# A two-layer streaming step on one core: eight state buffers, gate loads on GpSimd's queue, and two of four output shares beside the second layer's heads

## The chip, the cores and the metric

The kernel runs on one core of a Trainium2 chip. The metric is the time of one execution on the device, in microseconds; less is better. The core has TensorE (matrix products), VectorE, ScalarE and GpSimd, and queues from which transfers are issued; this kernel issues them from SyncE (SP) and from GpSimd. In the profile PE is TensorE's matmuls, PEld its weight loads, DVE is VectorE, ACT is ScalarE, POOL is GpSimd.

## The reference

Two streams of tokens go through two layers with the same weights: a prompt of 512 tokens, and 8 running sequences with 16 new tokens each, 640 tokens in all, 2048 wide, in float32. Layer 0 is stick-breaking attention with 16 heads; layer 1, where most of the change lies, is gated linear attention (GLA) with 4 heads, keys 256 wide and values 512 wide. Its core, cut:

```python
def gla_chunk(S, inp):
    q, k, v, g = inp                                   # g = log of the decay
    b = jnp.cumsum(g, axis=1)
    b_last = b[:, -1]
    q_in = q * jnp.exp(b)
    a = jnp.einsum('bchd,bshd->bhcs', q_in, k * jnp.exp(-b))
    a = jnp.where(tril, a, 0.0)
    o = jnp.einsum('bhcs,bshe->bche', a, v) + jnp.einsum('bchd,bhde->bche', q_in, S)
    S = jnp.exp(b_last)[..., None] * S + jnp.einsum('bshd,bshe->bhde', k * jnp.exp(b_last[:, None] - b), v)
    return S, o
...
    o = o * lax.rsqrt(jnp.mean(o * o, axis=-1, keepdims=True) + EPS) * g_out
    y = (o.reshape(B, T, nv) * jax.nn.silu(r)).astype(h.dtype) @ w_out
...
        x = x + gate[:, None] * y
    return rmsnorm(x, final_norm_g), ...
```

The 8 running sequences start from a given state (8 x 4 heads x 256 x 512 floats, 16.8 MB), which is read, used and written back updated. The prompt starts from zero, and its last state is an output too.

## The kernel before

**Products in three parts.** Each float32 factor is split into a high part (a cast to the matmul's reduced float32, on ScalarE) and a low part (the rest, by a subtraction on VectorE): `halves`, L134 to L136. A product is then three matmuls: high by high, high by low, low by high. A weight piece of 128 x 1024 is loaded into one of two raw buffers (`wraw`, tag `wr`) and split into one of three pairs `wh`, `wl` (`split`, L140; the third pair comes from a pool of its own at every third call, counted by `ring3["n"]`).

**Who sets the order.** TensorE's order is that of the program text. The text is made by a small planner: a main product is a generator that yields every few matmuls, and at each yield `Side.tick` (L305) lets side lanes run, which are generators too. A lane says with `step(wait, tp=...)` how many planned microseconds it wants to wait and how many PSUM banks it needs; planned time (`pe["now"]`) advances with the matmuls written. `side.after(wait, what)` puts a call, a transfer mostly, on a list of due calls, which is served from its head. The order on the other engines and on the queues is chosen by the compiler's scheduler, except in a stretch around the end of layer 0 and the start of layer 1 (L1157 to L1271), where VectorE, ScalarE and GpSimd follow the text as well. `load` and `store` (L70, L73) issue on SP's queue, `move` (L76) on GpSimd's.

**Layer 0's output product** is cut into four shares, one for each four of the 16 row blocks of the contraction (`share`, L603). A share goes through four columns of 512. In a column, tokens 0 to 2 are accumulated one after the other over both weight pieces (w0 and w1), then tokens 3 and 4 side by side. `made()` (L630) splits the next raw piece: before, the second piece of a column is split at the start of that column (L635), the first piece of the next one right after. Shares 0 to 2 add into `y_t`; share 3 (L1162) adds the residual, stores x1, and squares for the norm.

**Layer 1's projections.** `six` (L434) makes head 0's values in six token tiles; its first weight piece is loaded when it is first run (L1199), after the last token's norm. `add_up` (L408) makes the sums of activation quarters that the seven-product scheme (`by_sevens`, L456) needs; two of its four subtractions run on GpSimd.

**The heads' stage** (L1281 to L1658). The main product is first `others` (L1308), the queries and keys of heads 2 and 3: 768 matmuls of 320 columns. Beside it run four lanes. `decays` (L1390) turns the gate's projection into exponentials and scales q and k of a head. `prompt_lane` (L1444) runs 16 units, 4 heads by 4 chunks of 128 tokens: attention within the chunk (L1350), transposed keys (L1485), the incoming state S times a decay, split into S1h and S1l for both halves of the key width (L1489 to L1494), the output o (L1504 to L1507), its norm, the update of S (L1509 to L1517), and, two steps into the next unit, the turned and gated rows (`leave`, L1378: transposes at L1382, the gate's product, a move to `og_d`). `sample_lane` (L1545) does the 8 sequences for each head: 16 state tiles of 128 x 512 in four groups of four. For each group there are four products with the states (L1597), then four updates (L1603, L1605), whose left factors `kst` are brought together by moves through DRAM; each state is then moved out and the next one asked for (`leaves`, L1540: after 1.5 planned us, and 3.0 more). There are S0 = 5 state buffers and, for the prompt's gates, GP = 1. `fetches` (L1613) loads the finished rows of a head, four row blocks of 128 x 640, and splits them into `og1`.

When `others` is done, the shares of layer 1's output product run as filler between the lanes' steps: share g needs the rows of head g. Shares 0 to 2 run in the heads' stage (L1652), where the third one ends after the lanes.

**The tail** (L1661 to L1731) is share 3: 240 matmuls in groups of tokens (0, 1, 2), (3,), (4,) over all four columns, with all its weights split ahead into buffers of their own; then `add` (L1679): y added, times the layer's gate, plus x1, squared, times the final norm's weights (on GpSimd, L1688, in columns 0 to 2), and in the last column the norm of the token and its stores. `hs_gemm512` (L340) is a product over several row blocks, all five tokens accumulating at once; it stands in the file and isn't called.

Of the kernel before, what the change touches and what calls it, by code (L numbers as in the profile page):

```python
# [15 lines left out]
P = 128  # L16
# [17 lines left out]
S0 = 5  # L34
GP = 1
# [6 lines left out]
def hybrid_step_kernel(ctx: ExitStack, tc: tile.TileContext, A: dict, O: list):  # L42
# [391 lines left out]
    def six(h, w, n0, acc, until, asked):  # L434

        src = w.rearrange("(kt p) n -> p kt n", p=P)
# [5 lines left out]
        nxt = piece(0)  # L442
        for j in range(8):
# [159 lines left out]
    def share(g, og, w, leave=None, at=None, first=None):  # L603
# [29 lines left out]
        w0 = made()  # L633
        for c in range(4):
            ws = [w0, made()]  # L635
# [475 lines left out]
    with tc.tile_pool(name="o0", bufs=1, reuse_waits="tile") as po, ExitStack() as only_d:  # L1111
# [51 lines left out]
        ring3.update(pool=None, tags=("wh", "wl"))  # L1163
        side.finish()
# [27 lines left out]
        acc = [bank("mm") for _ in range(5)] + [bank("z")]  # L1192

        def until(j):
            make(j + 1)
            if j == 6:
                halves(wa[:, :, :16], wa[:, :, 16:], r)

        drive(six(h2, w_in1, 2 * NK, acc, until, lambda: None))  # L1199
# [72 lines left out]
        more.close()  # L1272
        ring3["pool"] = only_d.enter_context(tc.tile_pool(name="w2", bufs=1, reuse_waits="tile"))
# [18 lines left out]
    with tc.tile_pool(name="gl", bufs=1, reuse_waits="tile") as gl:  # L1292
# [37 lines left out]
        kst = [gl.tile([P, 4, 256], F32R, name=f"kst{n}") for n in range(2)]  # L1330
# [59 lines left out]
        def decays():  # L1390

            for h in range(GH):
# [15 lines left out]
                yield step(2.0)  # L1408
# [35 lines left out]
        def prompt_lane():  # L1444
# [16 lines left out]

            def leave_left():
# [6 lines left out]
            for u, (h, c) in enumerate(units):  # L1469
# [18 lines left out]
                if c:  # L1488
                    s1h, s1l = (gl.tile([P, 2, 512], F32R, tag=n, name=n) for n in ("S1h", "S1l"))  # L1489
                    s1 = [(s1h[:, dt, :], s1l[:, dt, :]) for dt in range(2)]  # L1490
                    for dt in range(2):
                        act(s1[dt][0], S[:, dt, :], AF.Copy, scale=e1[:, dt, c:c + 1])
                        dve.scalar_tensor_tensor(s1[dt][1], S[:, dt, :], e1[:, dt, c:c + 1],
                                                 s1[dt][0].bitcast(F32), op0=ALU.mult, op1=ALU.subtract)  # L1494
# [6 lines left out]
                yield step(6.0, tp=1)  # L1501
# [3 lines left out]
                if c:  # L1505
                    for dt in range(2):
                        mm3(o, [x[:, dt, :] for x in qc], s1[dt], False, dt == 1)  # L1507
# [13 lines left out]
                yield step(4.0)  # L1521
# [237 lines left out]
```

## Time and profile before

| | us |
|---|---|
| median of 3 runs | 2677.25 |
| the runs | 2669.66, 2677.41, 2677.25 |
| the profiled execution | 2672.06 |
| its span, first to last instruction | 2670.3 |
| PE busy, PEld busy | 2491.7, 2164.2 |
| DVE, ACT, POOL busy | 1617.4, 1018.9, 268.3 |
| heads' stage, first to last matmul | 2099 to 2583 |
| tail, to the end | 2583 to 2670 |

A row of the profile that groups instructions names the line, the engine, the operation, what is written and read, and a count; then the busy time, the mean of one, and the idle time of that engine just before them with its causes. A row of waits reads: engine, tile and line that waited, what ended the wait, the total in us, how often, the longest. A row of a timeline is the start, the length, engine, line and count, and in brackets the idle time ahead of it. PE's busy time is no measure of work by itself, since matmuls overlap.

### The profile page before, as it was taken

The page shows a single profiled execution, that of the slowest core. Times are in us where ns is not written, and L with a number is a line of the kernel's source. Part 1 is how long each engine was busy: PE and PEld are TensorE (multiplying, and loading weights), DVE is VectorE, ACT ScalarE, POOL GpSimd, SP SyncE. Part 2 cuts the span into 40 slices and gives each one's busy share as a digit, 9 for nine tenths or more (in the row PEclk, how much of TensorE's full clock was granted, in tenths as well). Part 3 has the DMA queues.
Part 4 walks back from the last instruction along what each step waited for, and adds up shares of the span by engine and source line. Part 5 has one row for each costly group of instructions (what it writes and reads, how often), then busy time and mean ns, then how long its engine had stood idle before and what let it go on. Part 6 is the DMA issues. An engine that isn't in the chain of part 4 may idle for free.

```text
span 2670.3 us, 43803 instructions
## 1 busy us (share of the span) xinstructions
PE 2491.7 (93%) x17393; PEld 2164.2 (81%) x17393; DVE 1617.4 (61%) x2426; ACT 1018.9 (38%) x1804; POOL 268.3 (10%) x516
## 2 busy tenths in 40 slices
PE   6989999999999989999999889999999998788986
PEld 4569999989999988777777667999999987566765
DVE  4555555555556646667775566666676563556557
ACT  4332222222223335665442353333333552543323
POOL 1200000000000000000000052000000233233113
PEclk8899999999999999999999889999999999899998
DMA  9966666766674366667665533334434667576444
GB/s 320 313 205 214 223 203 213 228 208 212 211 225 132 115 227 221 215 213 249 198 209 155 155 109 93 112 112 136 136 104 119 200 212 243 178 233 211 168 150 166
DMA packets 503552, 503.84 MB, mean 189 GB/s; under 512 B 25706, under 2 KB 426482, under 8 KB 503218
## 3 DMA queue, kind: packets, MB, share of 16 engines
q1 hardware_dynamic: 487986, 451.74, 53.9%
q0 software_dynamic: 15360, 49.30, 5.6%
q8 instruction: 137, 2.24, 0.4%
q14 instruction: 69, 0.57, 0.1%
HBM read 411.16 MB, written 89.78 MB: 188 GB/s over the span
## 4 chain that ended last, share of the span: by engine, by line
PE 72%; DMA 11%; DVE 7%; issue 5%; POOL 2%; ACT 2%; SPq 1%; POOLq 0%; ACTq 0%; DVEq 0%
PE ps_mm L518 40%; PE ps_mm L617 11%; PE ps_mm L452 4%; PE ps_mm L573 3%; PE ps_tp L972 2%; DMA s<-in_state_gla_dram 1%; DMA ar<-in_w_ada_dram 1%; PE ps_tp L940 1%; SPq L71 1%; PE ps_z L916 1%; PE ps_z L218 1%; DVE wl L136 1%; PE ps_z L178 1%; PE ps_tp L1017 1%; PE ps_z L985 1%
## 5 line engine op out<-in xcount | busy, mean ns | idle before, releaser
L518 PE MATMUL ps_mm<-sums,wh 128*128 128x320 f32 x2880 | 643.4, 312 | 4.3 <-ACT wh L135 4.3
L518 PEld LDWEIGHTS ps_mm<-sums,wh 128*128 128x128 f32 x2880 | 480.3, 188 | 16.3 <-issue 9.1
L518 PE MATMUL ps_mm<-h,wh 128*128 128x320 f32 x2160 | 483.2, 312 | 2.6 <-DVE u L524 2.0
L518 PE MATMUL ps_mm<-sums,wl 128*128 128x320 f32 x1440 | 446.4, 310 | 1.2 <-DVE wl L136 1.2
L136 DVE TENSOR_TENSOR wl<-wr,wh 128x1024 fp32r<-128x1024 f32 x195 | 240.8, 1236 | 234.3 <-ACT wh L135 233.6
L518 PEld LDWEIGHTS ps_mm<-h,wh 128*128 128x128 f32 x2160 | 359.1, 188 | 18.9 <-issue 11.3
L135 ACT CAST wh<-wb 128x1024 fp32r<-128x1024 f32 x180 | 188.9, 1049 | 463.7 <-PE ps_mm L518 387.3
L135 ACT CAST wh<-wr 128x1024 fp32r<-128x1024 f32 x195 | 204.3, 1049 | 374.5 <-PE ps_mm L518 199.3
L518 PE MATMUL ps_mm<-h,wl 128*128 128x320 f32 x1080 | 334.2, 309 | 0.7 <-DVE wl L136 0.7
L518 PEld LDWEIGHTS ps_mm<-sums,wl 128*128 128x128 f32 x1440 | 270.8, 188 | 1.8 <-DVE wl L136 1.8
L136 DVE TENSOR_TENSOR wl<-wb,wh 128x1024 fp32r<-128x1024 f32 x180 | 220.1, 1223 | 62.4 <-ACT wh L135 62.2
L617 PE MATMUL ps_mm<-wh,ogh 128*128 128x512 f32 x530 | 231.5, 437 | 21.7 <-ACT ogh L135 14.7
L617 PE MATMUL ps_mm<-wl,ogh 128*128 128x512 f32 x530 | 212.4, 401 | 1.3 <-DVE wl L136 1.3
L617 PE MATMUL ps_mm<-wh,ogl 128*128 128x512 f32 x530 | 211.8, 400 | 0.6 <-DVE ogl L136 0.4
L573 PE MATMUL ps_mm<-h,wh 128*128 128x320 f32 x896 | 209.7, 322 | 2.4 <-DVE out L524 2.4
L518 PEld LDWEIGHTS ps_mm<-h,wl 128*128 128x128 f32 x1080 | 202.8, 188 | 1.0 <-DVE wl L136 1.0
L573 PEld LDWEIGHTS ps_mm<-h,wh 128*128 128x128 f32 x896 | 153.7, 194 | 14.8 <-issue 10.6
L617 PEld LDWEIGHTS ps_mm<-wh,ogh 128*128 128x128 f32 x530 | 102.6, 193 | 52.8 <-ACT ogh L135 15.9
L573 PE MATMUL ps_mm<-h,wl 128*128 128x320 f32 x448 | 141.3, 315 | 3.9 <-DVE wl L136 3.9
L452 PE MATMUL ps_mm<-wh,h 128*128 128x512 f32 (+1 forms) x320 | 113.1, 424 | 13.8 <-ACT wh L135 5.9
L617 PEld LDWEIGHTS ps_mm<-wh,ogl 128*128 128x128 f32 x530 | 101.9, 192 | 25.0 <-DVE ogl L136 1.8
L617 PEld LDWEIGHTS ps_mm<-wl,ogh 128*128 128x128 f32 x530 | 102.6, 194 | 16.0 <-DVE wl L136 2.1
(296 smaller groups left out, 3811.4 us busy)
## 6 DMA issues: line engine op xcount, KB each, us to landing
ar<-in_w_ada_dram SPq DMA_DIRECT2D x160, 512.0 KB
wb<-in_sb_w_in_dram SPq DMA_DIRECT2D x84, 512.0 KB
kc<-in_cache_sb_k_dram SPq DMA_DIRECT2D x64, 512.0 KB
vc<-in_cache_sb_v_dram SPq DMA_DIRECT2D x64, 512.0 KB
wb<-in_gla_w_in_dram SPq DMA_DIRECT2D x51, 512.0 KB
wr<-in_gla_w_in_dram SPq DMA_DIRECT2D x45, 512.0 KB
wr<-in_sb_w_in_dram SPq DMA_DIRECT2D x44, 512.0 KB
ar<-in_w_ada_dram SPq DMA_DIRECT2D x64, 256.0 KB
```

The costliest lines, as they stand in the source:

```text
L71: nc.sync.dma_start(out=out, in_=in_)
L135: nc.scalar.copy(hi, x)
L136: dve.tensor_tensor(lo, x, hi.bitcast(F32), op=ALU.subtract)
L178: mm(acc[32 * q:32 * q + 32, :w], cT[:, kt + m, :], by(cT[:, kt + m, :], rs[m // each][:, m % each, q, :]), start=kt + m == 0, stop=kt + m ...
L218: mm(acc[32 * j:32 * j + 32, :256], cT[:, kt + m, :], by(cT[:, kt + m, :], r[:, 256 * j:256 * j + 256]), start=kt + m == 0, stop=kt + m == ...
L452: mm(acc[i][:n, :], l, by(l, r[:, e, :]), start=j == 0 and e == 0 and first, stop=j == 7 and e == 1 and last)
L518: mm(acc, l[:, k, :], by(l[:, k, :], r), start=start and k == 0 and first, stop=k == 7 and last, skip_group_check=True)
L573: mm(acc[nt], l[:, k, :], by(l[:, k, :], r), start=k0 == 8 and k == 0 and first, stop=k0 == 0 and k == 7 and last)
L617: mm(acc, l, by(l, r[:, e, :]), start=i == 0 and e == 0 and first, stop=i == 1 and e == 1 and last)
L916: mm(z[:, :n], q[:, hh, qs], by(q[:, hh, qs], k[:, hh, :n]), start=True, stop=True)
L940: mm(o[:, :P], l, by(l, aT[:, kb, :]), start=kb == 0, stop=kb == qb)
L972: turn_block(tp[:, P * c:P * c + P], block(kc[:, c, P * hh:P * hh + P]), ident)
```

## The change

Six edits, in the order of the file.

1. `share` (both layers): the second weight piece of the next column is split right after the first piece's products of tokens 3 and 4, not at the next column's start.
2. `six` yields once after its first piece; for layer 1 it is created and run to that point ahead of `side.finish()`, so the piece's load and split stand earlier. One of `add_up`'s two GpSimd subtractions goes to VectorE, and the count of the weight ring is set before the seven-product scheme.
3. Heads' stage, buffers and queues: S0 = 8, GP = 2; gates are loaded with `move` (GpSimd's queue) instead of `load` (SP's). S1h, S1l and kst are half as large: the second half of S1 is made after the first half's products, and kst's second half is moved in after the first two groups. States are asked for in the order in which the groups now come, 8.0 instead of 3.0 planned us after their store was due.
4. Steps of the lanes are changed: in `decays` ahead of L1417 5.0 for 2.0; in the sample lane ahead of L1573 6.0 for 3.0; in a prompt unit ahead of o 4.0 for 6.0, at its end 0.5 for 4.0, and a new 3.0 between the halves of S1.
5. Two shares instead of three in the heads' stage; `fetches` brings 14 of 16 row blocks.
6. The tail accumulates the last two heads' rows (row blocks 8 to 15) at once: columns 0 to 2 by `hs_gemm512`, the last one token by token with its weights split ahead; all of `add`'s products are on VectorE.

```diff
-S0 = 5
-GP = 1
+S0 = 8
+GP = 2
...
         nxt = piece(0)
+        yield
         for j in range(8):
...
-        w0 = made()
+        w0, w1 = made(), made()
         for c in range(4):
-            ws = [w0, made()]
+            ws = [w0, w1]
             if c < 3:
                 raws += [raw(c + 1, 0), raw(c + 1, 1)]
                 w0 = made()
...
+                    if i == 0 and c < 3:
+                        w1 = made()
...
+        acc = [bank("mm") for _ in range(5)] + [bank("z")]
+        gemm = six(h2, w_in1, 2 * NK, acc, until, lambda: None)
+        next(gemm)
         side.finish()
...
-                h2.add_up(j, pm, places[j], (0, 2))
+                h2.add_up(j, pm, places[j], (0,))
...
+        ring3["n"] = 2
...
-        kst = [gl.tile([P, 4, 256], F32R, name=f"kst{n}") for n in range(2)]
+        kst = [gl.tile([P, 4, P], F32R, name=f"kst{n}") for n in range(2)]
...
-            load(g, gr_d[h][:, :, t0:t0 + P])
+            move(g, gr_d[h][:, :, t0:t0 + P])
...
-                yield step(2.0)
+                yield step(5.0)
...
+            def state(S, e1, dt, c):
+                s1 = [gl.tile([P, 512], F32R, tag=n, name=n) for n in ("S1h", "S1l")]
+                act(s1[0], S[:, dt, :], AF.Copy, scale=e1[:, dt, c:c + 1])
+                dve.scalar_tensor_tensor(s1[1], S[:, dt, :], e1[:, dt, c:c + 1], s1[0].bitcast(F32),
+                                         op0=ALU.mult, op1=ALU.subtract)
+                return s1
...
-                yield step(6.0, tp=1)
+                yield step(4.0, tp=1)
                 v = vs.pop(u)
                 o = bank("tp")
                 mm3(o, a, v, True, c == 0)
                 if c:
-                    for dt in range(2):
-                        mm3(o, [x[:, dt, :] for x in qc], s1[dt], False, dt == 1)
+                    mm3(o, [x[:, 0, :] for x in qc], s1, False, False)
+                    s1 = state(S, e1, 1, c)
+                    yield step(3.0)
+                    mm3(o, [x[:, 1, :] for x in qc], s1, False, True)
...
-                yield step(4.0)
+                yield step(0.5)
...
-        wanted = [(h, e, dt, m) for h in range(GH) for e in range(2) for dt in range(2) for m in range(4)]
+        wanted = [(h, e, dt, m) for h in range(GH) for dt in range(2) for e in range(2) for m in range(4)]
...
-            side.after(3.0, ask)
+            side.after(8.0, ask)
...
-                yield step(3.0, tp=1)
+                yield step(6.0, tp=1)
...
+                def stack(e, dt):
                     for i in range(3):
-                        rows = st_d[h][int(i == 2)].rearrange("(m e t) n -> e t m n", m=4, e=2)[e]
+                        rows = st_d[h][int(i == 2)][:, P * dt:P * dt + P].rearrange("(m e t) n -> e t m n", m=4, e=2)[e]
                         r0 = 64 * e + NT * i
                         move(kst[e][r0:r0 + NT].bitcast(F32), rows)
+
+                for e in range(2):
+                    stack(e, 0)
...
+                    if n < 2:
+                        stack(e, 1)
...
-                return came["plain"] and came["shares"] >= (g if s > 1 else g - 1)
+                return came["plain"] and came["shares"] >= min(2, g if s > 1 else g - 1)
...
-            for kt in range(KT):
+            for kt in range(14):
...
-            for g in range(GH - 1):
+            for g in range(2):
...
+        for kt in (14, 15):
+            r = po.tile([P, T], F32, tag="rows", name="og_in", bufs=2)
+            load(r, og_d[3][:, kt - 12, :])
+            og1[kt] = [po.tile([P, T], F32R, name=f"og{n}{kt}") for n in "hl"]
+            halves(*og1[kt], r)
...
             if c < 3:
-                nc.gpsimd.tensor_tensor(y, y, gf[:, cs], op=ALU.mult)
+                dve.tensor_tensor(y, y, gf[:, cs], op=ALU.mult)
                 return
...
+        for c in range(3):
+            drive(hs_gemm512(og1, w_out1, 512 * c, lambda a, pt: add(a, c, pt), lambda: fetch_x1(c), piece=piece,
+                             k0=8, nk=8))
+        for i in range(4):
+            r = wraw(w_of(2 + i // 2, 3, i % 2), 2, 512)
+            h, lo = (po.tile([P, 1024], F32R, name=f"{n}{i}") for n in ("kh", "kl"))
+            halves(h, lo, r)
+            kept.append([t.rearrange("p (a n) -> p a n", a=2) for t in (h, lo)])
+        fetch_x1(3)
+        for a in range(TOK):
+            acc = bank("mm")
+            for n in range(8):
+                wh, wl = kept[n // 2]
+                h, lo = (x[:, P * a:P * a + P] for x in og1[8 + n])
+                for l, r, start, stop in ((h, wh, True, False), (h, wl, False, False), (lo, wh, False, True)):
+                    mm(acc, l, by(l, r[:, n % 2, :]), start=n == 0 and start, stop=n == 7 and stop)
+            add(a, 3, acc)
```

`fetch_x1` now loads a column's five tiles of x1 and its gates at once, with the final norm's weights before the first.

More of the change, by code (lines that the diff above doesn't have):

```diff
@@ L1163, in hybrid_step_kernel, with until @@
         ring3.update(pool=None, tags=("wh", "wl"))
+        def until(j):
+            make(j + 1)
+            if j == 6:
+                halves(wa[:, :, :16], wa[:, :, 16:], r)
+        acc = [bank("mm") for _ in range(5)] + [bank("z")]
+        gemm = six(h2, w_in1, 2 * NK, acc, until, lambda: None)
+        next(gemm)
         side.finish()
@@ L1191, in hybrid_step_kernel @@
         make(0)
[L1192 to L1199, printed above, removed]
+        drive(gemm)
         low = [bank("tp") for _ in hs]
@@ L1488, in prompt_lane @@
                 if c:
-                    s1h, s1l = (gl.tile([P, 2, 512], F32R, tag=n, name=n) for n in ("S1h", "S1l"))
-                    s1 = [(s1h[:, dt, :], s1l[:, dt, :]) for dt in range(2)]
-                    for dt in range(2):
-                        act(s1[dt][0], S[:, dt, :], AF.Copy, scale=e1[:, dt, c:c + 1])
-                        dve.scalar_tensor_tensor(s1[dt][1], S[:, dt, :], e1[:, dt, c:c + 1],
-                                                 s1[dt][0].bitcast(F32), op0=ALU.mult, op1=ALU.subtract)
+                    s1 = state(S, e1, 0, c)
                     qc = [gl.tile([P, 2, P], F32R, tag=n, name=n, bufs=1) for n in ("qch", "qcl")]
@@ L1638, in fetches @@
                 halves(*og1[kt], rows.pop(kt))
-                if kt % 4 < 3 and kt + 1 not in rows:
+                if kt % 4 < 3 and kt < 13 and kt + 1 not in rows:
                     ask_rows(kt + 1)
@@ L1664, in hybrid_step_kernel, with fetch_x1 @@
         gf = po.tile([P, D], F32, name="gf")
[L1665 to L1677 removed]
+        ring3["pool"] = po
+        for kt in (14, 15):
[3 more added lines that the diff above has]
+            halves(*og1[kt], r)
+        got = {}
+        def fetch_x1(c):
+            if c == 0:
+                load(gf, A["final_norm_g"].partition_broadcast(P))
+            xs = []
+            for a in range(TOK):
+                xs.append(po.tile([P, 512], F32, tag="xc", name="x1", bufs=8))
+                load(xs[a], x1_d[a][:, 512 * c:512 * c + 512])
+            got[c] = xs, gate_bc(po, 1, c)
         def add(a, c, pt):
             cs = slice(512 * c, 512 * c + 512)
+            xs, g = got[c]
             y = y_t[a, c]
             dve.tensor_tensor(y, pt, y, op=ALU.add)
[L1683 to L1684 removed]
+            dve.tensor_tensor(y, y, g[:, a // 4, :], op=ALU.mult)
+            dve.tensor_tensor(y, y, xs[a], op=ALU.add)
             junk = po.tile([P, 512], BF16, tag="junk", name="junk", bufs=1)
@@ L1702, in add @@
                 store(dst[:, 512 * n:512 * n + 512], x)
-        groups = ((0, 1, 2), (3,), (4,))
-        todo = [(a, c) for toks in groups for c in range(4) for a in toks]
-        for i in range(2):
-            weights(0, i)
-        gates[0] = gate_bc(po, 1, 0, 4)
-        load(gf, A["final_norm_g"].partition_broadcast(P))
-        for x in todo[:6]:
-            fetch_x1(*x)
-        ahead = iter(todo[6:])
-        for toks in groups:
-            for c in range(4):
-                if toks[0] == 0 and c < 3:
-                    for i in range(2):
-                        weights(c + 1, i)
-                    gates[c + 1] = gate_bc(po, 1, c + 1, 4)
-                for a in toks:
-                    acc = bank("mm")
-                    for i in range(2):
-                        wh, wl = ws[c, i]
-                        for e in range(2):
-                            h, lo = (x[:, P * a:P * a + P] for x in og1[KT - 4 + 2 * i + e])
-                            for l, r, first_, last_ in ((h, wh, True, False), (h, wl, False, False), (lo, wh, False, True)):
-                                mm(acc, l, by(l, r[:, e, :]), start=i == 0 and e == 0 and first_,
-                                   stop=i == 1 and e == 1 and last_)
-                    add(a, c, acc)
-                    x = next(ahead, None)
-                    if x:
-                        fetch_x1(*x)
@@ new lines, in piece @@
+        def piece(src, a, n):
+            if first:
+                return [t.rearrange("p (a n) -> p a n", a=2) for t in split(first.pop(0))]
+            return wpiece(src, a, n)
+        kept = []
+        for c in range(3):
[6 more added lines that the diff above has]
+            kept.append([t.rearrange("p (a n) -> p a n", a=2) for t in (h, lo)])
```

22 lines of the change are left out of this document (4 added, 18 removed).

## The prediction

> **What bounds the kernel now.** I read the page first, then busy time by stretches, then the waits of the heads' stage, then its timeline. The first TensorE instruction of the heads' stage (L573) starts at 2099 and its last one (L617 of the third share) at 2582; the tail (L1726) follows.
>
> ```profile
> span 2670.3 us, 43803 instructions
> PE 72%; DMA 11%; DVE 7%; issue 5%; POOL 2%; ACT 2%; SPq 1%; POOLq 0%; ACTq 0%; DVEq 0%
> ```
> ```profile
> 2099.00:2297.00 198.00, 178.62 (x1030) 153.06 (x1030) 99.14 (x174) 86.30 (x163) 66.19 (x125) 0.95 0.73 232
> 2297.00:2583.00 286.00, 251.61 (x1095) 188.20 (x1094) 156.16 (x266) 120.42 (x219) 67.78 (x118) 0.96 0.57 182
> 2583.00:2671.00 88.00, 59.33 (x240) 45.95 (x240) 66.34 (x90) 27.82 (x57) 26.02 (x20) 0.87 0.55 186
> ```
>
> TensorE carries the chain (72%). In the heads' stage (first two rows: length, then PE, PEld, DVE, ACT and POOL busy, clock, DMA share, GB/s) it is busy 430 of 484 us; in the tail 59 of 88. VectorE, ScalarE and GpSimd are far from full. So the stage is TensorE's work plus waits. Who ends them:
>
> ```profile
> PE ps_z L1597 <- DMA s<-in_state_gla_dram: 25.8, 18, 4.0
> PE ps_mm L617 <- ACT ogh L135: 12.4, 2, 11.6
> PE ps_tp L1573 <- DVE kd L1566: 5.7, 2, 5.1
> PE ps_tp L1417 <- DVE wa L1404: 4.4, 1, 4.4
> PEld ps_z L1597 <- DMA s<-in_state_gla_dram: 45.4, 26, 4.9
> SPq L71 <- DMA og<-gate: 132.9, 18, 20.3
> SPq L71 <- DVE wl L136: 112.3, 22, 19.5
> POOL s L78 <- DMA out_dram<-s: 44.8, 25, 4.3
> ```
>
> Half of TensorE's idle time is for states. GpSimd's queue stands 45 us in front of a state load whose buffer is still being stored, and SP's queue stands 133 us in front of a gate load whose only buffer is still being stored: weights, values and rows queue behind it.
>
> **The change part by part.**
>
> *The share that moves.* Share 2 (240 matmuls of 512 columns) leaves the stage; the tail's 240 become 480. The chain has 27 such matmuls in 6.23 us, 0.231 each: 55.4 us out of the stage, 55.4 into the tail. Added up this is nothing; the stage gives them back only if the lanes can also end earlier.
>
> ```profile
> 2488.85 6.23 PE ps_mm L617 x27
> 2432.71 1.06 PE L1597 MATMUL ps_z<-s,qz 128*32 128x512 f32 x8
> 2474.31 1.06 PE L1597 MATMUL ps_z<-s,qz 128*32 128x512 f32 x6
> 2478.80 1.92 PE L1597 MATMUL ps_z<-s,qz 128*32 128x512 f32 x2 [3.43 <-DMA s<-in_state_gla_dram]
> ```
>
> *State waits.* A group with its states there takes 1.06 us (first L1597 row); the group at 2474 took until 2480.7, 6.4 us, of which only 3.43 shows as idle. So 25.8 us of idle cost more: between 25.8 and PEld's 45.4; I take 40, nearest to the second, since the matmuls between the waits are slowed as well. With eight buffers the first two groups of a head lie ready, and the load comes 8 us after its store was due instead of 3, so GpSimd no longer stands before a landing store. The list of due moves is served from its head (L307), so these 8 us also hold back later stores: groups three and four come about 20 us behind the first two. I leave 6 us of waits: 34 gained, between 15 and 40.
>
> *Rows, kd, wa.* Without gate loads SP's largest wait goes; next on SP is the slot of the raw weights (112 us), which stays. Share 0's stall (12.4) is rows 0 to 3 arriving one behind the other through two buffers; that half stays: 7 gained (0 to 12). The longer steps ahead of L1573 (6 for 3) and L1417 (5 for 2) let filler run where TensorE now waits 5.7 and 4.4: 9 gained together.
>
> *GpSimd's queue.* Twenty gate loads and 24 more, half as large, kst moves come in.
>
> ```profile
> L78 POOL DMA_DIRECT2D s<-in_state_gla_dram x64: 536/551/763, 2099.4 to 2473.2; - x64
> L78 POOL DMA_DIRECT2D og<-gate x20: 717/735/750, 2168.4 to 2569.6; - x20
> og<-gate POOLq DMA_DIRECT2D x20, 256.0 KB, 3.6
> L136 DVE TENSOR_TENSOR wl<-wr,wh 128x1024 fp32r<-128x1024 f32 x38 | 46.5, 1223 | 41.6 <-ACT wh L135 41.3
> ```
>
> At 0.735 and 0.55 us they are 28 us more on an engine busy 134 of 484: hidden. A gate load also waits for its buffer's store, which lands 3.6 us after issue; with two buffers it is due 4 us later, so it hardly waits. Behind it stand state loads and stores and the norms' powers (L230); their slack in the plan (7 us from load to use) covers 3.6 us. The Trainium skill (SBUF — State Buffer, section "SBUF: two separate sides") says that VectorE instructions of some kinds lock GpSimd out of a shared port, so that a DMA issued from GpSimd's queue waits for its descriptors, and advises the other queues. That speaks against this move; the issues' spread (717 to 750 ns) does not show it. It is a rival below.
>
> *The prompt lane.* Waits per unit fall from 14.1 to 11.6 us of the plan, and to 8.6 for a head's first unit. Units (the attention product L1350) of the last head, with the sample lane gone, come 20.0 and 18.4 us apart; from the first to the last head's first there are twelve in 343 us, 28.6 each.
>
> ```profile
> 2142.30 0.60 PE L1350 MATMUL ps_tp<-q,k 128*128 128x128 f32 x4
> 2485.04 0.60 PE L1350 MATMUL ps_tp<-q,k 128*128 128x128 f32 x4
> 2504.99 0.60 PE L1350 MATMUL ps_tp<-q,k 128*128 128x128 f32 x4
> 2523.43 0.61 PE L1350 MATMUL ps_tp<-q,k 128*128 128x128 f32 x4
> L1492 ACT ACTIVATE S1h<-S,e 128x512 fp32r<-128x512 f32 x24 | 17.3, 722 | 0.8 <-DVE S L1516 0.7
> L1493 DVE SCALAR_TENSOR_TENSOR S1l<-S,e,S1h 128x512 fp32r<-128x512 f32 x24 | 17.8, 747 | 0.8 <-ACT S1h L1492 0.7
> ```
>
> New: the second half of S1 is made only after the first half's products, in the same buffer: 0.72 + 0.75 us in sequence under a step of 3 us. When both engines are free it is covered; queued behind a weight split (1.22 us) it isn't. Twelve units: 0 to 15 us, I take 6. When the two shares are used up, the last one or two units run without filler at the latency of their chain: 0 to 30 us, I take 10.
>
> Stage: 484 − 55 − 34 − 7 − 9 + 16 = 395. As a check from the lane: 43 us to its first unit, then 16 units of 22 make 395. A unit of 22 is 19.2 (alone now, the mean of the two) less 3.3 (the steps' cut, on average), and 6 for the other lanes' work and waits, where it is 9 now.
>
> *Layer 0's last share.* At each column's end the split of the second weight piece stands on ScalarE behind the leaving tokens.
>
> ```profile
> PE ps_mm L617 <- ACT wh L135: 5.6, 2, 2.8
> PE ps_mm L617 <- ACT s L135: 2.8, 1, 2.8
> PE ps_mm L617 <- DVE wl L136: 1.3, 2, 0.8
> PE ps_mm L617 <- DVE s L136: 1.3, 2, 0.8
> PE ps_mm L452 <- ACT wh L135: 5.9, 1, 5.9
> PE ps_mm L518 <- ACT wh L135: 3.8, 1, 3.8
> L415 POOL TENSOR_TENSOR sx<-xp x16: 875/1122/5275, 1578.7 to 1665.2; 128x320 f32<-128x320 f32 x16
> L415 DVE TENSOR_TENSOR sx<-sx,xp x8: 479/480/1152, 1608.3 to 1665.3; 128x320 f32<-128x320 f32 x8
> ```
>
> The first four rows are 11.0 us; split ahead of tokens 3 and 4, all go. The early first piece of the values' product removes part of 5.9: the activations are cast just before it, so 2, or up to 4 lost if its load is late in an ordered queue. Eight subtractions leave GpSimd (1.12 us) for VectorE (0.48), 4 us more on a VectorE that is full there, against a 3.8 us wait that followed a GpSimd subtraction of 5.3: 0 ± 4. The order of states and the ring's count cost nothing. Together 13.
>
> *Tail.* 480 × 0.231 = 111; 3 us to start; 8 for weights behind gates, rows of x1 and the norm's weights (5.4 for a split now, below). In columns 0 to 2 five tokens leave within a piece's 6.9 us, while VectorE needs 4 × 0.68 = 2.7 for each, 14 in all, since the product with the norm's weights is now its own; the next column's 27.7 us of matmuls cover that, but splits can queue behind it: the 8 are 2 to 15. The rows of kt 14 and 15 are due only after three pieces, 3 × 30 × 0.231 = 21 us, which covers their store and load. After the last matmul come 13.1 us to the last VectorE result, since token 4's four columns pile up on VectorE, where L1684 takes 1.0 us beside GpSimd's products and L1682 0.68; then the store to 2670.3.
>
> ```profile
> PE ps_mm L1726 <- ACT wh L135: 5.4, 1, 5.4
> 2652.21 0.39 PE L1726 MATMUL ps_mm<-wh,ogl 128*128 128x512 f32 x1
> 2665.34 0.48 DVE L1701 TENSOR_SCALAR y<-y,fin_r 128x512 f32<-128x512 f32 x1
> L1684 DVE TENSOR_TENSOR y<-y,x 128x512 f32<-128x512 f32 x20 | 19.9, 1001 | 0.3
> L1682 DVE TENSOR_TENSOR y<-ps_mm,y 128x512 f32<-128x512 f32 x20 | 13.7, 683 | 6.6 <-PE ps_mm L1726 6.6
> ```
>
> After the change a token comes every 24 × 0.231 = 5.5 us and VectorE needs about 4, so nothing piles up: some 7 + 5 = 12 instead of 18. Tail: 111 + 3 + 8 + 12 = 134 (128 to 146).
>
> **Sum.** 2099 − 13 + 395 + 134 = 2615, and 2 around the span (the profiled execution took 2672.06): 2617 against 2672, 55 less. That execution lies 5 under the median of 2677.25, so on the median's scale 2622.
>
> **Rivals.**
> *GpSimd's issues are held by VectorE* (the page's rule). For: a GpSimd subtraction took 5.3 us for 0.9 beside VectorE. Against: the even issues. If each of the 44 new issues waits for one split (1.22 us), 54 us more stand in the queue that feeds the states, and their 34 us are not gained: 2656.
> *Transfers become the bound.* The stage moved 484 × 203 GB/s = 98 MB, now 4 less; in 395 us that is 238 GB/s on average, above the 232 of its busiest half. That half's DMA share of 0.73 speaks for room, the bursts of eight states against. At 220 GB/s the stage takes 427: 2654.
> *The lanes set the stage* (slower). If units keep 26 us or more, taking filler away shortens nothing, because TensorE's order is the lanes' plan and each wait for S or a state comes in it. Break-even is a stage of 450 us, units of 25.4; with units as now the last rows turn at 2567.6, stage 470: 2697. Against: waits of the plan fall by 2.5 to 5.5 a unit.
> *All waits go*: none for states (6), rows (5), S1 (6) or at the end (10), stage 368: 2595.
> *Even trade*: stage of 442 to 458, between 2669 and 2685.
>
> **How the numbers follow.** Forecast (stage 375 to 418, 2602 to 2645) 0.55; GpSimd held 0.10; transfers 0.12; lanes 0.10; all waits 0.08; even 0.05. What differs by under 0.3% (8 us) can't be told from no change here. Faster: 0.55 + 0.10 + 0.12 + 0.08 = 0.85; slower 0.10, same 0.05. Range 2582 to 2666: low enough for the good case with the tail at its short bound, high enough for the two middle rivals with 10 us more; it leaves out the lanes, the even trade and what lies beyond those bounds. The forecast's own: 2602 to 2645.
>
> **What would show it.** Right: state waits on TensorE under 10 us in all, no og<-gate wait on SP, unit spacing near 22 us, the tail's first matmul near 2480, 13 us less by 2099, L617's column waits gone in layer 0. Wrong: units of 25 us or more, waits of L1597 as long as now, GpSimd issues over 1 us, or a tail over 146 us.

## The result and the profile after

| | before | after |
|---|---|---|
| median, runs of both on one chip | 2675.21 | 2632.45 |
| lowest to highest | 2669.66 to 2677.41 | 2632.06 to 2633.23 |
| profiled span | 2670.3 | 2631.4 |
| heads' stage, first matmul to the tail's first | 2099.1 to 2584.2, 485.1 | 2086.6 to 2510.3, 423.8 |
| tail | 86.1 | 121.1 |

The ratio is 0.9844, 95% interval 0.9827 to 0.9861: 42.8 us less, where 55 were forecast. By parts of the span: 12.5 us less up to the heads' stage (forecast 13), a stage of 424 (forecast 395) and a tail of 121 (forecast 134). Lines move: L573 is now L575, L617 L619, L1597 L1613, L1603 L1619, L1492 and L1493 L1472 and L1473, L1573 L1585, L1350 L1357; the tail is L356 and L1747.

From the page of the kernel after, its span and the chain that ended last:

```profile
span 2631.4 us, 43839 instructions
PE 74%; DMA 7%; DVE 7%; issue 5%; ACT 3%; POOL 3%; SPq 1%; ACTq 0%; POOLq 0%; DVEq 0%
```

TensorE still carries the chain; the share of DMA fell from 11 to 7%. Busy time by stretches (length, then PE, PEld, DVE, ACT, POOL busy, clock, DMA share, GB/s), two for the heads' stage and one for the tail:

```profile
2086.60:2280.00 193.40, 173.37 (x1047) 152.55 (x1048) 100.17 (x177) 85.98 (x165) 82.68 (x148) 0.94 0.77 245
2280.00:2510.00 230.00, 189.10 (x839) 143.00 (x837) 131.80 (x233) 110.10 (x206) 77.67 (x133) 0.93 0.58 194
2510.00:2632.00 122.00, 111.08 (x480) 90.10 (x480) 73.35 (x114) 37.87 (x68) 3.47 (x6) 0.98 0.54 181
```

The tail is now nearly all matmuls, 111 of 122 us. The stage is not: 61 of 423 us are idle, and the clock is lower than before (0.94 and 0.93 for 0.95 and 0.96). Who ends the waits of the stage:

```profile
PE ps_tp L1619 <- DMA kst<-k: 22.8, 3, 11.0
PE ps_mm L619 <- ACT ogh L135: 8.7, 2, 7.8
PE ps_tp L1389 <- ACT on L1371: 7.7, 4, 2.7
PE ps_tp L1345 <- ACT S1h L1472: 5.9, 1, 5.9
PE ps_z L1613 <- DMA s<-in_state_gla_dram: 5.3, 5, 2.0
PEld ps_z L1613 <- DMA s<-in_state_gla_dram: 10.4, 6, 2.9
SPq L71 <- PE ps_tp L1345: 139.9, 12, 23.9
SPq L71 <- DVE wl L136: 83.2, 16, 14.9
SPq L71 <- DMA og<-gate: 29.6, 2, 23.8
POOL gate L78 <- DMA og<-gate: 14.7, 6, 3.0
```

The waits for states fell from 25.8 to 5.3 us. A wait that the forecast did not have took the first place: for `kst`, the sample lane's stacked key rows, 22.8 us, two of its three waits being about 10 and 11 us long. In the kernel before these products (L1603) waited only once, and for nothing that the view names:

```profile
PE ps_tp L1603 <- issue: 3.3, 1, 3.3
```

Where the second of the four heads waits is told by three views of the kernel after: the turning of the keys on TensorE, their split on VectorE, and GpSimd's queue behind that, in order of time (start, length, engine, what, idle time ahead):

```profile
2207.33 0.38 PE L1585 MATMUL ps_tp<-ident,kd 128*128 128x128 f32 x2
2229.08 0.76 PE L1619 MATMUL ps_tp<-vst,kst 128*128 128x512 f32 x1 [11.02 <-DMA kst<-k]
2231.24 0.63 PE L1619 MATMUL ps_tp<-vst,kst 128*128 128x512 f32 x1
2235.09 0.40 PE L1619 MATMUL ps_tp<-vst,kst 128*128 128x512 f32 x1
```
```profile
2208.15 0.42 DVE L136 TENSOR_TENSOR krl<-ps_tp,krh 128x256 fp32r<-128x256 f32 x1
```
```profile
2208.45 0.74 POOL L78 DMA_DIRECT2D og<-gate  x1 [5.30 <-DVE S1l L1473]
2214.07 0.72 POOL L78 DMA_DIRECT2D og<-gate  x1 [4.88 <-DVE S L1528]
...
2218.27 0.78 POOL L78 DMA_DIRECT2D gate<-gr  x1 [2.94 <-issue]
2219.04 0.55 POOL L78 DMA_DIRECT2D k<-krh  x1
2222.54 0.76 POOL L78 DMA_DIRECT2D gate<-gr  x1 [2.95 <-issue]
2223.29 0.55 POOL L78 DMA_DIRECT2D k<-krl  x1
...
2224.38 2.08 POOL L78 DMA_DIRECT2D kst<-k  x4
```

The key rows are split at 2208.6. Their low half is stored only at 2223.3: ahead of it in GpSimd's queue stand two stores of gated rows and two gate loads. The first store's wait of 5.3 us is over just before the split ends; the second store's 4.9 us and the loads' 2.9 us each fall in between, 10.8 of the 14.7 us. Then the way itself (stored to DRAM, loaded back) takes 5.8 us more. In the kernel before, the keys of this head were turned by 2216.9 and stored 1.8 us later, by the same two timelines, of TensorE and of GpSimd:

```profile
2216.56 0.38 PE L1573 MATMUL ps_tp<-ident,kd 128*128 128x128 f32 x2
```
```profile
2218.70 0.54 POOL L78 DMA_DIRECT2D k<-krl  x1 [0.41 <-DVE aT L1353]
```

### The profile page after: what moved, and what is told of

Its sections match the earlier page's. It is cut to its first block, busy times and chain, and to the rows that moved or that the text cites. A ratio compares the mean times of both kernels' runs of the same rounds, so it can differ in the third digit from the quotient of the medians.

```text
span 2631.4 us, 43839 instructions
## 1 busy us (share of the span) xinstructions
PE 2475.0 (94%) x17393; PEld 2162.9 (82%) x17393; DVE 1597.8 (61%) x2429; ACT 1017.4 (39%) x1804; POOL 261.3 (10%) x537
## 4 chain that ended last, share of the span: by engine, by line
PE 74%; DMA 7%; DVE 7%; issue 5%; ACT 3%; POOL 3%; SPq 1%; ACTq 0%; POOLq 0%; DVEq 0%
PE ps_mm L520 41%; PE ps_mm L619 8%; PE ps_mm L454 4%; PE ps_mm L356 3%; PE ps_mm L575 3%; PE ps_tp L976 2%; PE ps_tp L944 1%; PE ps_z L920 1%; PE ps_z L178 1%; DMA ar<-in_w_ada_dram 1%; PE ps_z L218 1%; DVE wl L136 1%; PE ps_tp L1021 1%; PE ps_mm L1747 1%; PE ps_z L989 1%
## 5 line engine op out<-in xcount | busy, mean ns | idle before, releaser
L520 PEld LDWEIGHTS ps_mm<-sums,wh 128*128 128x128 f32 x2880 | 479.4, 188 | 12.2 <-issue 9.0
L136 DVE TENSOR_TENSOR wl<-wr,wh 128x1024 fp32r<-128x1024 f32 x191 | 233.9, 1226 | 234.0 <-ACT wh L135 233.0
L619 PE MATMUL ps_mm<-wh,ogh 128*128 128x512 f32 x450 | 199.7, 444 | 15.5 <-ACT ogh L135 11.0
L575 PE MATMUL ps_mm<-h,wh 128*128 128x320 f32 x896 | 209.1, 321 | 3.5 <-DVE out L526 2.1
L619 PE MATMUL ps_mm<-wh,ogl 128*128 128x512 f32 x450 | 180.4, 401 | 0.6 <-DVE ogl L136 0.4
L619 PE MATMUL ps_mm<-wl,ogh 128*128 128x512 f32 x450 | 180.4, 401 | 0.0
L575 PEld LDWEIGHTS ps_mm<-h,wh 128*128 128x128 f32 x896 | 153.0, 193 | 16.0 <-issue 11.3
L575 PE MATMUL ps_mm<-h,wl 128*128 128x320 f32 x448 | 140.9, 315 | 2.3 <-DVE wl L136 2.3
L454 PE MATMUL ps_mm<-wh,h 128*128 128x512 f32 (+1 forms) x320 | 113.4, 425 | 10.0 <-ACT h L135 7.1
L619 PEld LDWEIGHTS ps_mm<-wh,ogh 128*128 128x128 f32 x450 | 87.8, 195 | 41.7 <-ACT ogh L135 12.2
L858 DVE TENSOR_TENSOR_SCAN k<-k,zero_c 128x544 f32<-128x544 f32 (+4 forms) x96 | 93.3, 975 | 29.7 <-ACT k L854 17.5
L619 PEld LDWEIGHTS ps_mm<-wh,ogl 128*128 128x128 f32 x450 | 86.6, 192 | 21.7 <-DVE ogl L136 1.8
```

What stands on the lines that cost most here:

```text
L136: dve.tensor_tensor(lo, x, hi.bitcast(F32), op=ALU.subtract)
L454: mm(acc[i][:n, :], l, by(l, r[:, e, :]), start=j == 0 and e == 0 and first, stop=j == 7 and e == 1 and last)
L520: mm(acc, l[:, k, :], by(l[:, k, :], r), start=start and k == 0 and first, stop=k == 7 and last, skip_group_check=True)
L575: mm(acc[nt], l[:, k, :], by(l[:, k, :], r), start=k0 == 8 and k == 0 and first, stop=k0 == 0 and k == 7 and last)
L619: mm(acc, l, by(l, r[:, e, :]), start=i == 0 and e == 0 and first, stop=i == 1 and e == 1 and last)
L858: dve.tensor_tensor_scan(kr, kr, zeros[:, :w], 1.0, ALU.mult, ALU.add)
```

## The experiments

Every kernel's ratio (in brackets, with its 95% interval) is to the kernel before on the same chip, which ran at 2671.4 to 2672.7 us; at its ratio of 0.9844 the kernel after stands at 2630 to 2631 there, and what follows is set against that. "Theory A" is at first: the eight buffers made the gain, and the wait for `kst` is what gates in GpSimd's queue cost.

**Gates back on SP**, with two buffers.

```diff
-            move(g, gr_d[h][:, :, t0:t0 + P])
+            load(g, gr_d[h][:, :, t0:t0 + P])
```


> The changed kernel with the gates loaded from SP's queue again (two buffers stay); TensorE's order is the same. Theory A: TensorE's new wait for kst (22.8 us in three places, two of them 11.0 and 10.0) comes from gate loads that stand in GpSimd's queue between the moves of k and those of kst, each waiting about 3 us for the store of the gate's buffer. Then kst waits fall to under 6 us, no GpSimd wait for a gate's store is left, and the time falls by 15 to 25 us, to about 2612. Rival B: the kst wait comes from kst's halved buffers and its 24 more moves; then it stays at 18 to 25 us and the time stays within 6 us of 2632. Rival C: SP's queue stands before the gates again as in the kernel before (132.9 us there); then rows and weights come late, the waits for ogh and wh grow by 15 us or more, and the time rises to 2640 or more.

Measured 2621.81 (ratio 0.9814, 0.9798 to 0.9831), 9 us faster than after. The wait for `kst` fell, but not to under 6. From the waits of its stage:

```profile
PE ps_tp L1619 <- DMA kst<-k: 15.0, 2, 11.0
```

The wait that keeps its 11.0 us is again that of the second head, by the timelines of GpSimd's queue and of TensorE:

```profile
2215.42 0.63 POOL L78 DMA_DIRECT2D k<-krl  x1
2219.88 3.09 POOL L78 DMA_DIRECT2D kst<-k  x6 [3.25 <-DMA k<-krh]
```
```profile
2227.62 0.77 PE L1619 MATMUL ps_tp<-vst,kst 128*128 128x512 f32 x1 [11.03 <-DMA kst<-k]
```

Without the gate loads the low half is stored 8 us earlier than in the kernel after, but the way takes 12.2 us instead of 5.8, so the products start only 1.5 us earlier. The gates are a part of what stands ahead of the key rows, not all of it. On SP they wait 101.7 us for the stores of their buffers; TensorE's waits for rows hardly change (9.6 us for 8.7).

**Only the sample lane's gate on SP.**

```diff
-            move(g, gr_d[h][:, :, t0:t0 + P])
+            (load if tag == "gn" else move)(g, gr_d[h][:, :, t0:t0 + P])
```


> The changed kernel with only the sample lane's gate (four loads, one buffer) loaded from SP's queue; the prompt's sixteen stay with GpSimd. Theory A: of the two gate loads that hold up k and kst at 2218 and 2222, the one that waits for the sample lane's own store goes and the prompt's stays, so about half of the kst wait goes: 8 to 14 us left, time about 2622. Rival B (halved kst buffers): kst waits stay at 18 to 25 us, time within 6 us of 2632. Rival C: a sample gate on SP waits for the store of the head before, which is late, and holds SP for 10 us or more per head; rows and values come late and the time rises.

Measured 2626.47 (0.9834, 0.9817 to 0.985), `kst` wait 14.4 us. Four of twenty gates give the same shortening of that wait as all of them; in time it can't be told from either neighbour.

**Five state buffers**, the next state asked for after 3.0.

```diff
-S0 = 8
+S0 = 5
...
-            side.after(8.0, ask)
+            side.after(3.0, ask)
```


> The changed kernel with five state buffers and the next state asked for 3 planned us after its store, as before; the rest of the change stays. Theory A: the eight buffers are what took the waits for states from 25.8 to 5.3 us; with five they come back to 20 us or more and the time rises by 20 to 40 us, to 2652 to 2672. Rival D: the waits for states fell because gate loads left SP's queue or because the share left the stage; then they stay under 10 us and the time within 8 us of 2632.

Measured 2667.71 (0.9981, 0.9968 to 0.9994): 37 us slower than after, nearly all of the whole gain. The waits that the buffers remove come back, in the waits of TensorE and of GpSimd:

```profile
PE ps_z L1613 <- DMA s<-in_state_gla_dram: 47.7, 17, 5.2
POOL s L78 <- DMA out_dram<-s: 35.8, 22, 3.7
```

The stage takes 464.3 us, 40.5 more than after. By stretches, the whole stage with five buffers and then that of the kernel after:

```profile
2081.50:2545.80 464.30, 386.75 (x1885) 300.77 (x1885) 233.24 (x410) 196.78 (x371) 159.72 (x280) 0.90 0.62 198
```
```profile
2086.60:2510.30 423.70, 362.46 (x1884) 295.55 (x1884) 232.17 (x410) 196.08 (x371) 160.34 (x281) 0.93 0.67 217
```

The waits for states are 42.4 us longer, but TensorE's idle time in all grows by only 16.3 us (77.5 for 61.2), since the other waits, for `ogh`, `on` and S1h (22.3 us in the kernel after), are nearly gone. The other 24.3 us are slower matmuls, at a clock of 0.90 for 0.93. The run undoes the buffers and the later asking together; which of them did it wasn't tried apart.

**The new order of the splits alone**, in the kernel before.

```diff
-        w0 = made()
+        w0, w1 = made(), made()
...
-            ws = [w0, made()]
+            ws = [w0, w1]
...
+                    if i == 0 and c < 3:
+                        w1 = made()
```


> The kernel before with the new order of weight splits in the shares and nothing else. Theory A: the 11.0 us that TensorE waits for the second weight piece at the three column ends of layer 0's last share go, and some of the waits for row weights in the second layer's shares: 9 to 14 us less than before, about 2662. Rival E: the time goes back to the norm that follows (its tokens leave at the same time anyway), 0 to 4 us less.

Measured 2657.24 (0.9952, 0.9934 to 0.997), 13 to 15 us faster than before. Of L617's 11.0 us of waits on splits in layer 0's last share 0.6 is left in the view of the waits, and the stage begins at 2083.3 instead of 2099.1. The first edit is worth what was said. In the kernels with the same text up to the heads' stage that beginning varies from 2081.5 to 2087.9, so 15.8 here and 12.5 after can't be told apart.

After these four, 15 us of the `kst` wait had no owner: GpSimd's queue without the gates, or the way of the keys through DRAM itself. The next kernel takes the rows out of that queue.

**The key rows on SP**, gates left on GpSimd's queue.

```diff
-                    move(t, x.bitcast(F32))
+                    store(t, x.bitcast(F32))
...
-                        move(kst[e][r0:r0 + NT].bitcast(F32), rows)
+                        load(kst[e][r0:r0 + NT].bitcast(F32), rows)
```


> The kernel after, with the sample lane's key rows (k stored and kst loaded, 14 moves a head) on SP's queue; the gates stay in GpSimd's. What is left of the kst wait when the gates leave GpSimd (15.0 of 22.8 us) is the question. Theory A: GpSimd's queue delays them. In the kernel after the products with the gate at 2199 and 2201 are stored only at 2208 and 2214, the queue idle in between, and k and kst stand behind. On SP they don't, so the kst wait falls under 6 us and the time to 2615 to 2626. Rival E: the way itself is too long for the plan (kd turned, cast, stored, loaded: about 10 us at best) or SP, which stands 140 us for buffers of values, is no better: kst wait of 12 or more, 2628 to 2645.

Measured 2601.88 (0.9736, 0.9716 to 0.9756): 29 us faster than after, more than any theory gave. No wait for `kst` is left. The same head in that kernel, by the timelines of TensorE and of SP's queue, and then busy time by stretches, the stage's two parts:

```profile
2198.39 0.38 PE L1585 MATMUL ps_tp<-ident,kd 128*128 128x128 f32 x2
2211.66 0.50 PE L1619 MATMUL ps_tp<-vst,kst 128*128 128x512 f32 x1 [2.54 <-ACT on L1371]
```
```profile
2199.84 0.43 SPq L74 DMA_DIRECT2D k<-krl  x1
2204.53 2.94 SPq L71 DMA_DIRECT2D kst<-k  x6
```
```profile
2087.00:2260.00 173.00, 164.94 (x1043) 146.75 (x1044) 99.40 (x178) 85.90 (x165) 68.99 (x120) 1.00 0.84 274
2260.00:2476.00 216.00, 185.38 (x842) 140.62 (x840) 131.19 (x233) 109.51 (x206) 63.79 (x105) 0.95 0.62 206
```

The store comes 1.1 us after the turning instead of 15.6. So it is the start of their way that GpSimd's queue held. The way itself isn't shown to be shorter on SP (from this store to the product 11.8 us, the last 2.5 of which wait for something else), and SP, which stands 82 us of this stage for the buffers of values, is early enough. The stage takes 389.3 us. The first rows show why 22.8 us of waits were worth 34: nearly the same matmuls (1043 and 1047) take 173.0 us instead of 193.4, of which 12.0 are less idle time (8.1 for 20.0) and 8.4 are faster matmuls (164.9 us busy for 173.4), at a clock of 1.00 for 0.94.

**The second edit undone**: the early first piece and the count of the weight ring taken out, both subtractions on GpSimd again.

```diff
-        gemm = six(h2, w_in1, 2 * NK, acc, until, lambda: None)
-        next(gemm)
...
-                h2.add_up(j, pm, places[j], (0,))
+                h2.add_up(j, pm, places[j], (0, 2))
...
-        ring3["n"] = 2
```


> The kernel after without its second edit (the first piece of the values' product is loaded where it was, both subtractions of add_up on GpSimd, the weight ring's count as before). Theory A: the second edit costs some 3 us, since the new split order alone brought the heads' stage forward by 15.8 us and the whole change only by 12.5: 2626 to 2631, stage begins 2 to 4 us earlier. Rival: the early piece is worth its 2 us as forecast: 2633 to 2637, a wait on wh ahead of L454 of about 6 us is back. Between the two lies no difference that can be told.

Measured 2650.55 (0.9916, 0.9895 to 0.9937): some 20 us slower, the opposite of theory A. But the stage begins at 2086.5, as after. The loss is behind it, where the text is the same but for the count. Two kernels split the edit.

**Only the ring's count left out.**

```diff
-        ring3["n"] = 2
```


> The kernel after without the one line that sets the weight ring's count to 2. Undoing the whole second edit made it 18 us slower, though the heads' stage then began within 1 us of where it does after; 10.3 us of it is one wait for a split weight at the tail's first matmul. Theory R: the count decides which of the three pairs each piece of the shares and of the tail gets, and the wait comes of that alone: 2643 to 2655, with a wait on wh of 8 us or more ahead of L356. Rival: the count costs nothing (as forecast) and the early piece or the subtraction made it: 2629 to 2636, no such wait.

Measured 2639.97 (0.989, 0.9872 to 0.9908), 10 us slower, 3 us under theory R's range. The largest wait around the stage's end:

```profile
PE ps_mm L356 <- ACT wh L135: 10.3, 1, 10.3
```

The count decides which of the three pairs of split weights each piece gets. Without it the split that releases the tail's first matmul stands on ScalarE at 2509.6, after the last filler (2499.9) and behind a split that waits 5.5 us for its raw weights and the splits of two row blocks, which wait 3.0 us for theirs. In the kernel after two splits for the tail stand on ScalarE ahead of it, at 2490.8 and 2506.2. That the piece's pair was not free earlier is read from the text; the views don't name the pairs. The prediction put the count at nothing.

**The second edit undone, with the count kept** (the first two parts of the diff above).

> The kernel after without the early first piece and with both subtractions on GpSimd, but with the weight ring's count set to 2 as after. Theory R: as fast as after, 2628 to 2637, since only the count mattered; the heads' stage begins within 2 us of 2086. Rival: the early piece or the subtraction is worth the 18 us: 2643 to 2655.

Measured 2633.6 (0.9855, 0.9837 to 0.9874): no difference from after. The wait on wh at L454 (L453 here) is back with 5.5 us, and one of L241 is 3.1 instead of 6.1 us: the two take each other up. What remains open is why the count costs 10 us alone and 20 together with the other two parts; in the second case the waits for `on` are 13.6 us too, where they are 7.7 after.

**Three shares in the heads' stage**, tail and `fetches` as before, the rest as after.

```diff
-            for g in range(2):
+            for g in range(GH - 1):
...
```


> The kernel after with three shares in the heads' stage and the tail of before; buffers, queues and steps stay changed. Theory A: with the filler lasting to the stage's end, the third share adds its 55 us to the stage whole, and the tail goes from 121 back to about 88: 2645 to 2658, some 20 us slower than after; the move is worth the tail's gain alone. Rival F (the move only trades matmuls, the tail's gain is eaten): 2628 to 2640. Rival C (lanes set the stage, so filler fills their waits): stage under 455 and 2605 to 2628.

Measured 2654.46 (0.994, 0.9922 to 0.9959), 23 us slower than after. The third share makes the stage 62 us longer (486.0 for 423.8) and the tail 38 us shorter (83.3 for 121.1).

**Two shares and the new tail alone**, in the kernel before.

```diff
-            for g in range(GH - 1):
+            for g in range(2):
...
```


> The kernel before with only the last share moved and the new tail; five state buffers, gates on SP, old steps and old split order. Theory A: the move needs the shorter steps and the buffers. The lanes' last rows turn at 2568 in the kernel before, so the stage shrinks by 15 to 25 us only and filler runs out; the tail grows by about 33 less: 2670 to 2690, no gain. Rival G (the parts add up): stage 429 (484 less 55), tail 121: 2645 to 2657.

Measured 2670.47 (0.9993, 0.9979 to 1.0007): no difference. The stage gives 41 us (444.3 for 485.1) and the tail takes 37. Here the filler runs out: its last matmul ends at 2511, 33 us ahead of the tail. By the timeline the last units come 10 to 11 us apart, and the tail waits for its weights:

```profile
2503.50 0.60 PE L1350 MATMUL ps_tp<-q,k 128*128 128x128 f32 x4
2514.29 0.61 PE L1350 MATMUL ps_tp<-q,k 128*128 128x128 f32 x4
2524.73 0.61 PE L1350 MATMUL ps_tp<-q,k 128*128 128x128 f32 x4
2543.52 0.80 PE L356 MATMUL ps_mm<-wh,ogh 128*128 128x512 f32 x1 [9.59 <-ACT wh L135]
```

The time came out as theory A said; its figure for the stage (15 to 25 us shorter) didn't. The ring's count is not set in this kernel, and the wait of 9.6 us is of the kind that the count removed above; the move with the count alone wasn't tried.

**A longer step at a unit's end**, 4.0 for 0.5, in the kernel after.

```diff
-                yield step(0.5)
+                yield step(4.0)
```


> The kernel after with 4.0 instead of 0.5 planned us at the end of a prompt unit (its planned waits rise from 11.6 to 15.1 us). Theory A, as in the prediction: units of the plan set when the lanes end, and two shares of filler are only just enough; 16 units of 3.5 us more are 56 us of plan, so the filler runs out before the lanes, and the last units run bare: 2645 to 2675. Rival: TensorE's work and its waits set the stage and the plan has room: 2628 to 2638.

Measured 2621.67 (0.9811, 0.9792 to 0.9831): 8 us faster, where theory A said 15 to 45 slower. The filler does run out before the lanes, at 2476, 28 us ahead of the tail, but the last units then follow each other in 9 us:

```profile
2473.11 0.61 PE L1357 MATMUL ps_tp<-q,k 128*128 128x128 f32 x4
2482.28 0.61 PE L1357 MATMUL ps_tp<-q,k 128*128 128x128 f32 x4
2491.13 0.61 PE L1357 MATMUL ps_tp<-q,k 128*128 128x128 f32 x4
```

A bare unit is short, since nothing lies between its steps; what it leaves idle (some 3 us of 9) is less than what the longer spacing saves before: the waits on `kst` are 14.9 us instead of 22.8, those on `on` 1.7 instead of 7.7. Up to the last head the units come 27.0 us apart, where they are 24.0 in the kernel after, and the stage is still 7 us shorter (417.2).

**Gates and key rows both on SP** (the diffs of the first and the fifth kernel together).

> Both moved to SP: the gate loads and the sample lane's key rows; GpSimd's queue has the states, vst, the gated rows and heads 2 and 3's queries and keys alone. Theory A: with the key rows on SP the gates no longer hold anything up on GpSimd, and on SP they stand again ahead of weights and key rows: the same as with the key rows alone, or slower: 2598 to 2612. Rival: every transfer taken from GpSimd's queue is worth something (10 us for the gates alone): 2588 to 2597.

Measured 2602.14 (0.9733, 0.9715 to 0.9751): as with the key rows alone (one wait for `kst`, 4.5 us, is back). Once the key rows are out of GpSimd's queue, it no longer matters where the gates are. These two kernels beat both before and after.

## Why the prediction was right, and where not

The time lies in the range, 10 us above the forecast, and the main mechanism was right: the states' waits made the gain, and the move of the share adds its part only beside the other edits. The stage came out 29 us longer than forecast and the tail 13 shorter; that the second miss takes up part of the first is luck. Point by point:

- *State waits*: 34 forecast (15 to 40), with 6 left. 5.3 us are left, and five buffers, asked for as before, cost 37. So the size came out. The price of 40 us for 25.8 of waits isn't measured by it as a figure, but its reason is borne out: with five buffers 16.3 us more of idle time made the stage 40.5 us longer, the rest being slower matmuls.
- *GpSimd's queue*: this step failed. It counted 28 us more of issues as hidden, and the issues are as short as it took them (0.52 us for a kst move, 0.77 for a gate load; 0.55 and 0.735 forecast). But it said that a gate load hardly waits, and the twenty wait 14.7 us for stored rows and 40.6 us more for nothing that the view names. And it looked at what stands behind them: states and norms, with slack. The key rows stand there too, and they have none. Price: the 22.8 us of waits, and 29 us of the time, which the key rows gain by leaving that queue. Only 9 us come back when the gates leave it; the rest stands with the stores of gated rows and the way through DRAM, and why these came to hold the key rows after the change stays open. With the key rows on SP the stage is 389, where 395 was forecast.
- *Rows*: 7 us forecast, with 5 of 12.4 left; 8.7 left, 4 gained. *kd and wa*: 9 forecast, with nothing left; 0.7 left.
- *S1's second half*: 6 us forecast, 5.9 in a single wait. *End without filler*: 10 us forecast, none needed, since the filler lasted.
- *Layer 0's last share*: 11.0 us forecast, 10.4 of the waits gone. *The early piece*: 2 forecast, nothing found. *The ring's count*: nothing forecast, 10 us found. 
- *Tail*: 134 forecast, 121 measured. The 480 matmuls take the 111 us of the forecast. The 8 us for weights behind other transfers and the 3 to start are not there (one wait of 1.4 us ahead of the first matmul), and the last token takes 10 us instead of 12. VectorE keeps up as reckoned; from the groups of the tail, its four products (mean in ns after the busy time):

```profile
L1704 DVE TENSOR_TENSOR y<-ps_mm,y 128x512 f32<-128x512 f32 x20 | 13.6, 682 | 1.2 <-PE ps_mm L1747 1.2
L1705 DVE TENSOR_TENSOR y<-y,gate_bc 128x512 f32<-128x512 f32 x20 | 13.6, 683 | 0.1
L1706 DVE TENSOR_TENSOR y<-y,x 128x512 f32<-128x512 f32 x20 | 13.5, 684 | 0.2
L1710 DVE TENSOR_TENSOR y<-y,gf 128x512 f32<-128x512 f32 x15 | 10.0, 682 | 0.0
```

With GpSimd's products gone, the addition of x1 takes 0.68 us, where it took 1.00 before; that the one made the other wasn't tried apart.

- *The share that moves*: neutral by itself, as forecast (though with the wait of 9.6 us for weights, which the ring's count might remove); with the other edits it is worth 23 us (62 off the stage, 38 on the tail), since the third share costs the stage 7 us more than its matmuls, and since the tail that grew is free of waits.

The rivals. *GpSimd's issues held by VectorE*: the row of all kst moves in the kernel after is even, beside a VectorE that is busy half of the time.

```profile
L78 POOL DMA_DIRECT2D kst<-k x48: 512/518/553, 2142.9 to 2441.2; - x48
L78 POOL DMA_DIRECT2D gate<-gr x20: 747/772/795, 2094.2 to 2479.3; - x20
```

The rule of the Trainium skill (SBUF — State Buffer, section "SBUF: two separate sides") on a lock of GpSimd by VectorE isn't seen in these rows. Nor does it account for the two gate loads that wait 2.9 us each at 2218 and 2222: VectorE ran nothing from 2213.7 to 2225.7. What the other waits under "issue" were isn't shown. The advice of the Trainium skill there, to issue from another queue, paid, but for another reason: the key rows' store no longer stands behind other transfers. *Transfers become the bound*: no; the key rows on SP let the first part move 274 GB/s at a DMA share of 0.84, above the 245 of after. *The lanes set the stage*: the longer step made the kernel faster, so this falls, and with it the reckoning from units of 22 or 26 us: units of 24.0 us gave a stage of 424 and units of 27.0 one of 417. The plan's waits seem only to say how much filler lies in a unit. *All waits go*: a stage of 368 was its mark; 389 is the best that ran. *Even trade*: a stage of 442 to 458 was its mark, and it took 424.

What was to show it right: states under 10 us, yes; units near 22 us, no, 24.0 (twelve in 287.7 us); the tail's first matmul near 2480, no, 2510; no wait of SP for stored rows, nearly (29.6 of 132.9 us remain, for other loads than the gates'); 13 us less by 2099 and L617's column waits gone, yes. Of the signs of being wrong (units of 25 us, waits for states as before, issues over 1 us, a tail over 146) none came.

## What to carry to other kernels

When a transfer is moved to another queue, list what stands behind it there and the slack of each, the last link of a chain above all: the waits of issues ahead of it, not their durations, made the price. A wait of 10 us on TensorE can cost more than 10 us, because the matmuls after it are slower. A counter that hands out buffers in turn is part of the schedule: after a change that shifts it, look at who waits for which buffer.

## What the runs showed of the hardware

TensorE's matmuls are slower for some us after a pause. In the kernel after, matmuls of 128x512 that take 0.39 to 0.40 us as recorded took 0.76 behind the 11.0 us wait at 2229, 0.63 two us later, and 0.40 again at 2235; between them three matmuls of 320 columns (L575) started every 0.80 us until 2233.3, and every 0.43 from 2234.2. Shorter pauses can do it too: behind the wait of 3.43 us at 2478.80 in the kernel before, 128x512 took 0.63 us until 2484.2. Behind the one of 2.54 us at 2211.66 with the key rows on SP it took 0.39 at 2212.9. The Trainium skill (TensorE: Matmul & The Clock Gate, section "Part 1: The HAM clock gate") says that the array runs at half its clock after an idle window of about 3.4 us, until it has been busy for one; the rows agree with the half, with about 5 us until full speed here. In all, the stage without the wait for key rows was granted a clock of 1.00 in its first part, where 0.94 was granted with it.

What held the two stores of gated rows at 2208 and 2214, whose products on VectorE had ended by 2201.6, isn't settled: the trace names VectorE's S1l and S as what ended the waits, which these stores don't read.
